# An encoder layer on one core: weights traced two pairs ahead, the up projection in the order of the source, and the heavy pair first in the last block

## The chip, the cores and the metric

The kernel runs on one core of one Trainium2 chip. The metric is the device time of one execution in microseconds (us): 1366.28, the median of three runs from 1365.36 to 1366.99. The engines are PE (TensorE), DVE (VectorE), ACT (ScalarE), POOL (GpSimd) and SP (SyncE, which here only issues transfers).

## The reference

One layer of a bidirectional encoder for 256 tokens and a model width of 2048, in float32: a combined input projection, two attention branches with sigmoid gates, an output projection with a residual, and an MLP of width 8192 with a squared ReLU.

```python
proj = jnp.einsum('bsd,dc->bsc', rms_norm(x, norm_mix_pre[l]), w_in[l])
qa, ka, va, qn, kn, vn, gates = jnp.split(proj, split_at, axis=-1)
...
g_a, g_b = jnp.split(jax.nn.sigmoid(gates), N_BRANCHES, axis=-1)
mixed = (g_a * jnp.einsum('bsc,cd->bsd', oa, w_branch_a[l])
         + g_b * jnp.einsum('bsc,cd->bsd', on, w_branch_b[l]))
y = jnp.einsum('bsd,de->bse', mixed, w_out[l])
x = x + rms_norm(y, norm_mix_post[l])
h = rms_norm(x, norm_mlp_pre[l])
u = jnp.square(jax.nn.relu(jnp.einsum('bsd,df->bsf', h, w_up[l])))
x = x + rms_norm(jnp.einsum('bsf,fd->bsd', u, w_down[l]), norm_mlp_post[l])
```

## The kernel before

Every matrix product is made of three: operands are split into a high part (float32r) and a low part, and high x high, high x low and low x high are summed in PSUM. `pair_weights` (L602) loads 1 MB of weights, a *pair* of row blocks by 1024 columns, into `raw`, casts it to the high part on ACT (tiles ending in `h`, L609) and subtracts to get the low part on DVE (`l`, L610). Raw, high and low tiles have three slots each. A name such as `u_1h` is the high part of pair 1 of the up projection `u`; with numbers kept, `u2_1h` belongs to its third group.

A pair is used in one of two ways (`Products`, L632). A *plain* pair takes 24 matmuls of 512 columns (`eight`). A *heavy* pair is multiplied with seven products instead of eight (`seven`, L655): 21 matmuls, but DVE must first make sums of its blocks (`t`, L614 to L616) and split these too (`eh`, `el`, L626 and L627). Its products go to sums numbered 0 to 6 in PSUM, which `combine` (L673) joins at the end. Sums 1, 2, 3 and 7 have four banks of their own; sums 0, 4, 6 and 5 share four small banks (pool `ms`) with the transposes.

The up projection (L1030 to L1062) has eight groups of 1024 columns with eight pairs each. The first group takes plain pairs only; it begins while the residual of the stage ahead is still being made: `residual_parts` (L865) computes `x` on DVE, PE transposes it (`h2T_t`), and ACT and DVE write the high and low part of the pieces `h2T` (L885, L886) that the pairs are multiplied with. The other groups have two heavy pairs. While a group runs, the result of the one before is transposed on PE (`uT`, L1014, four banks in all, two for each half), squared on ACT (L1017), split into `ah` and `al`, with sums `sm` for the heavy use, and stored to DRAM (`u_sets`, L1006).

The down projection (L1105 to L1164) makes two halves of 1024 output columns from blocks of four pairs; the saved parts come back through ACT's queue as `bh` and `bl` (L989). A pair `d1131` is half 1, column group 13, part 1. The last block of a half ends with combining the heavy sums into `zw` (L677 to L680), adding the plain sums, and in the second half scaling and storing the result.

A scheduler sets the order of each engine's instructions: it goes by the order in which they are traced and by which it expects to be ready. `issue_after` keeps an instruction behind another one of its engine. Only the last blocks of the down projection have PE in the order of the source (`pr.in_order`, L1114).

## Time and profile before

| | |
|---|---|
| median of three runs | 1366.28 us |
| profiled execution, own time | 1367.36 us |
| its span, first to last instruction | 1365.5 us |
| mean granted clock of TensorE | 0.995 |
| stages: input projection and attention / gates and branches | to about 305 / 305 to 568 us |
| output projection / up / down | 568 to 658 / 658 to 1016 / 1016 to 1354 us |

The page has the busy time of each engine, a chain followed back from the last instruction, and groups of instructions with their mean duration and the idle time before them. Matmuls overlap, so the pace is read from starts. The granted clock is the share of TensorE's full clock that the throttle let through. Lines like L649 are lines of the kernel before.

### The profile page before, as it was taken

What the parts mean: (1) busy time and instruction counts of PE and PEld (TensorE: products, weight loads), DVE (VectorE), ACT (ScalarE), POOL (GpSimd) and SP (SyncE); (2) the same over time, 40 slices, a digit from 0 to 9 for tenths busy, and PEclk for the clock granted to TensorE, in tenths of its full rate; (3) what the DMA queues carried; (4) which work ended last, traced back from release to release, by engine and by line L of the source; (5) the groups of instructions that cost most, each with busy time, mean ns of one, the idle gap of its engine ahead of it and who ended that gap; (6) DMA issues with size and microseconds to landing.
All of it is one profiled execution on the core that took longest, in us unless ns stands there. A gap on an engine that the chain in (4) does not pass through costs nothing.

```text
span 1365.5 us, 16240 instructions
## 1 busy us (share of the span) xinstructions
PE 1341.8 (98%) x6350; PEld 1122.6 (82%) x6350; DVE 1030.8 (75%) x1176; ACT 716.4 (52%) x841; POOL 36.2 (3%) x71
## 2 busy tenths in 40 slices
PE   7999999999999999999999999999999999999995
PEld 6888888888888888888788888888888888888884
DVE  6868866667857886654768877888788888798885
ACT  7555455555644464444465655666555555555451
POOL 0000000000000000000100000000000000000000
PEclk9999999999999999999999999999999999999997
DMA  9674745564556655676567776786699999698992
GB/s 310 201 227 165 205 158 178 163 206 154 185 186 215 216 185 185 205 265 203 197 206 268 252 245 244 258 280 238 249 339 356 374 353 358 248 387 310 373 356 75
DMA packets 116397, 333.76 MB, mean 244 GB/s; under 512 B 17248, under 2 KB 18528, under 8 KB 116320
## 3 DMA queue, kind: packets, MB, share of 16 engines
q1 hardware_dynamic: 96784, 264.03, 56.7%
q10 hardware_dynamic: 12816, 43.01, 8.1%
q0 software_dynamic: 6720, 25.69, 4.8%
q8 instruction: 50, 0.82, 0.2%
q14 instruction: 27, 0.22, 0.0%
HBM read 304.91 MB, written 29.61 MB: 245 GB/s over the span
## 4 chain that ended last, share of the span: by engine, by line
PE 61%; issue 34%; DVE 2%; DMA 2%; ACT 1%; ACTq 0%; SPq 0%; POOL 0%; DVEq 0%; POOLq 0%
PE u L649 25%; PE p L649 22%; PE qa_p L192 2%; PE ka_p L192 2%; DMA bl<-keepl 1%; PE qa_p L193 1%; PE ka_p L193 1%; PE qn_p L192 1%; PE va_p L230 1%; PE va_p L231 1%; PE va_p L232 1%; PE uT L1014 1%; PE qn_p L193 1%; PE ds L378 0%; PE do L378 0%
## 5 line engine op out<-in xcount | busy, mean ns | idle before, releaser
L117 DVE TENSOR_TENSOR y_l<-y_w,y_h 128x1024 fp32r<-128x1024 f32 x32 | 37.9, 1222 | 31.0 <-ACT y_h L116 31.0
L116 ACT CAST y_h<-y_w 128x1024 fp32r<-128x1024 f32 x32 | 32.1, 1052 | 40.9 <-PE y_p L232 32.5
L230 PE MATMUL y_p<-y_h,mh 128*128 128x512 f32 x128 | 50.1, 391 | 0.0
L231 PE MATMUL y_p<-y_l,mh 128*128 128x512 f32 x128 | 49.9, 390 | 0.0
L232 PE MATMUL y_p<-y_h,ml 128*128 128x512 f32 x128 | 49.8, 390 | 0.0
L192 PE MATMUL qa_p<-hT,qa_h 128*128 128x512 f32 x128 | 46.9, 411 | 1.2 <-DVE hT L275 1.2
L649 PE MATMUL u<-u_0h,h2T 128*128 128x512 f32 x128 | 44.6, 392 | 2.3 <-DVE ry_m L86 1.1
L192 PE MATMUL qn_p<-hT,qn_h 128*128 128x512 f32 x128 | 45.9, 400 | 0.0
L192 PE MATMUL kn_p<-hT,kn_h 128*128 128x512 f32 x128 | 45.4, 398 | 0.0
L192 PE MATMUL ka_p<-hT,ka_h 128*128 128x512 f32 x128 | 45.0, 398 | 0.0
L649 PE MATMUL u<-u_1h,h2T 128*128 128x512 f32 x128 | 44.6, 395 | 0.0
L649 PE MATMUL u<-u_4h,h2T 128*128 128x512 f32 x128 | 42.1, 390 | 0.0
L649 PE MATMUL u<-u_2h,h2T 128*128 128x512 f32 x128 | 41.9, 397 | 0.0
L649 PE MATMUL u<-u_6h,h2T 128*128 128x512 f32 x128 | 41.8, 389 | 0.0
L649 PE MATMUL u<-u_7h,h2T 128*128 128x512 f32 x128 | 41.0, 389 | 0.0
L193 PE MATMUL qn_p<-hT,qn_l 128*128 128x256 f32 x128 | 35.9, 281 | 0.0
L193 PE MATMUL kn_p<-hT,kn_l 128*128 128x256 f32 x128 | 35.7, 280 | 0.0
L193 PE MATMUL qa_p<-hT,qa_l 128*128 128x256 f32 x128 | 35.2, 285 | 0.0
L193 PE MATMUL ka_p<-hT,ka_l 128*128 128x256 f32 x128 | 35.2, 280 | 0.0
L609 ACT CAST u_1h<-u_1r 128x2048 fp32r<-128x2048 f32 x8 | 15.3, 1917 | 36.0 <-PE u L649 32.5
L649 PEld LDWEIGHTS u<-u_0h,h2T 128*128 128x128 f32 x128 | 23.9, 188 | 8.4 <-DVE ry_m L86 1.6
L192 PEld LDWEIGHTS qa_p<-hT,qa_h 128*128 128x128 f32 x128 | 24.5, 194 | 6.6 <-DVE hT L275 1.6
(1376 smaller groups left out, 4351.2 us busy)
## 6 DMA issues: line engine op xcount, KB each, us to landing
y_w<-in_w_out SPq DMA_DIRECT2D x16, 1024.0 KB, 5.2
bh<-keeph ACTq DMA_DIRECT2D x30, 512.0 KB, 9.6
bl<-keepl ACTq DMA_DIRECT2D x30, 512.0 KB, 11.6
keeph<-ah POOLq DMA_DIRECT2D x18, 512.0 KB, 3.5
keepl<-al POOLq DMA_DIRECT2D x18, 512.0 KB, 7.2
ka_w<-in_w_in SPq DMA_DIRECT2D x8, 1024.0 KB, 5.7
va_w<-in_w_in SPq DMA_DIRECT2D x8, 1024.0 KB, 5.1
qn_w<-in_w_in SPq DMA_DIRECT2D x8, 1024.0 KB, 5.2
```

Of the source, the lines that this page charges most:

```text
L116: nc.scalar.copy(hi[part], raw[part])
L117: nc.vector.tensor_sub(lo[part], raw[part], hi[part].bitcast(F32))
L192: nc.tensor.matmul(ps[b], hi[:, k % 4, cs], mv, start=(k == 0), stop=False)
L193: nc.tensor.matmul(ps[b][:, :T], lo[:, k % 4, cs], mv[:, :T], start=False, stop=(k == nk - 1))
L230: nc.tensor.matmul(ps[t], sh, hi[:, k % 4], start=(k == 0), stop=False)
L231: nc.tensor.matmul(ps[t], sh, lo[:, k % 4], start=False, stop=False)
L232: nc.tensor.matmul(ps[t], sl, hi[:, k % 4], start=False, stop=(k == nk - 1))
L609: nc.scalar.copy(h1, raw)
L649: ins = nc.tensor.matmul(self.ps[i], st, mv[:, blk], start=i not in self.begun, stop=last and n == 2).ins
L1014: nc.tensor.transpose(pt[:, j * T + t * P : j * T + (t + 1) * P], z[t][:, cg % 2, c : c + P], ident)
```

## The change

Weights are asked for in a list ahead of the loop, one list for gates and branches (`gw`), one for the up and down projections together (`uw`). `next` hands out one pair and has the two behind it traced first, so that their load, cast and subtraction are traced ahead of the work in between; that work (`each`) now comes behind the call. In `seven`, sum 0 moves behind 2 and 1. In the up projection the heavy pairs are 0 and 3 (before 3 and 5), at the third and fifth place (before fourth and sixth), and PE keeps the order of the source from the second group on. In the first group the low parts of pairs 1 and 2 are put behind named instructions of DVE. The last block of each half of the down projection begins with its heavy pair.

```diff
-    def pair_weights(view, name, seven, low=None):
+    def pair_weights(view, name, seven, low=None, after=None):
...
-            nc.vector.tensor_sub(l1, raw, h1.bitcast(F32))
+            with tc.issue_after(after) if after else nullcontext():
+                nc.vector.tensor_sub(l1, raw, h1.bitcast(F32))
...
+    class Weights:
...
+        def next(self, after={}):
+            i = self.used = getattr(self, "used", -1) + 1
+            upto = min(i + 3, len(self.asked), self.stop or len(self.asked))
+            for n in range(len(self.got), max(upto, i + 1)):
+                self.got.append(pair_weights(*self.asked[n], after=after.get(n)))
+            w, self.got[i] = self.got[i], None
+            return w
...
-            self.add(0, stat(0), r, 1, last)
             self.add(2, stat(6), r, 2)
             self.add(1, stat(1), r, 3)
+            self.add(0, stat(0), r, 1, last)
...
+        pr.in_order = in_order
         for n, (i, seven) in enumerate(kinds):
+            w = weights.next(after)
             if each:
                 each(n)
-            w = pair_weights(view(i), f"{name}_{i}", seven)
...
-    UPS = [(0, 0), (1, 0), (2, 0), (3, 1), (4, 0), (5, 1), (6, 0), (7, 0)]
+    UPS = [(1, 0), (2, 0), (0, 1), (4, 0), (3, 1), (5, 0), (6, 0), (7, 0)]
...
+    def down_steps(g, bi):
+        b = blocks[g][bi]
+        if bi == 0:
+            return [(b + 1, 0, 0), (b, 1, 0), (b, 0, g), (b + 1, 1, 0)]
+        return [(b, 0, 1), (b + 1, 0, 0), (b, 1, bi < len(blocks[g]) - 1), (b + 1, 1, 0)]
...
-                    for i in (3, 5):
+                    for i in (0, 3):
...
-            turn=None if g else partial(residual_parts, 1, 0),
+            turn=None if g else turn_rows,
+            after={} if g else {1: tail[1][1], 2: scaled[0]},
+            in_order=g > 0,
...
-            elif end:
-                steps = [(b + 1, 0, 0), (b, 0, 1), (b, 1, 0), (b + 1, 1, 0)]
-                pr.in_order = True
...
+            pr.in_order = end
```

(`tail[1][1]` is the last low piece of `residual_parts` for the first 128 tokens, `scaled[0]` the scaling `ry_m` for the second 128.)

PE in the third group of the up projection, where the heavy pair's sums begin (`u20` to `u27` are the sums of this group; `uT30` and `uT31` are transposes of the second half of the group before). Before:

```order
L649 MATMUL u20_6347<-u2_5h_6404,h2T5_4852 128x512 [waits Activation_49]
L649 MATMUL u22_6190<-u2_5h_6404,h2s5_5798 128x512
L649 MATMUL u21_6183<-u2_5h_6404,h2T5_4852 128x512
L649 MATMUL u24_6357<-u2_3eh0_6339,h2s3_5787 128x512 [waits PE_49,Activation_49]
L649 MATMUL u26_6361<-u2_3eh0_6339,h2s3_5787 128x512
L649 MATMUL u20_6347<-u2_5l_6405,h2T5_4852 128x512 [waits DVE_49]
L649 MATMUL u20_6347<-u2_5h_6404,h2T5_4852 128x512
L649 MATMUL u22_6190<-u2_5l_6405,h2s5_5798 128x512
L649 MATMUL u22_6190<-u2_5h_6404,h2s5_5798 128x512
L649 MATMUL u21_6183<-u2_5l_6405,h2T5_4852 128x512
L649 MATMUL u21_6183<-u2_5h_6404,h2T5_4852 128x512
```

Now:

```order
L686 MATMUL u20_6346<-u2_0h_6189,h2T0_4847 128x512 [waits Activation_49]
L686 MATMUL u20_6346<-u2_0l_6190,h2T0_4847 128x512
L686 MATMUL u20_6346<-u2_0h_6189,h2T0_4847 128x512
L686 MATMUL u24_6350<-u2_0eh0_6198,h2s0_5803 128x512 [waits Activation_49]
L686 MATMUL u24_6350<-u2_0el0_6199,h2s0_5803 128x512
L686 MATMUL u24_6350<-u2_0eh0_6198,h2s0_5803 128x512
L686 MATMUL u26_6354<-u2_0eh0_6198,h2s0_5803 128x512 [waits PE_49,Activation_49]
L686 MATMUL u26_6354<-u2_0el0_6199,h2s0_5803 128x512
L686 MATMUL u26_6354<-u2_0eh0_6198,h2s0_5803 128x512
L686 MATMUL u25_6358<-u2_0eh1_6202,h2s0_5803 128x512 [waits PE_49,Activation_49]
L686 MATMUL u25_6358<-u2_0el1_6203,h2s0_5803 128x512
```

In both built programs sum 6 (`u26`) takes the bank of `uT30` and waits for PE and ACT. Before, some 47 matmuls, of two plain pairs and of both heavy ones, stood between the last of the four transposed banks and sum 4 (`u24`) with sum 6 behind it; now twelve matmuls of the heavy pair stand between the transposes and sum 6.

ACT in the same group, from the cast of the pair `u2_3` to the squares of the second half, `u3<-uT30` and `u3<-uT31`. Before:

```order
L613 CAST u2_3h_6330<-u2_3r_6328 128x1536 [waits DMAHW3_49,PE_49,Activation_49]
L1017 ACTIVATE u2_6211<-uT20_6212 128x512 [waits PE_49]
L1017 ACTIVATE u2_6211<-uT21_6218 128x512 [waits PE_49]
L972 CAST ah20_6229<-u2_6211 128x256 [waits Activation_49]
L972 CAST ah20_6229<-u2_6211 128x512 [waits Activation_49]
L972 CAST ah21_6239<-sm2_6224 128x1024 [waits DMASW5_49,DMASW1_49,DVE_49]
L609 CAST u2_4h_6374<-u2_4r_6372 128x2048 [waits DMAHW4_49,PE_49]
L1017 ACTIVATE u3_6277<-uT30_6278 128x512 [waits DMASW6_49]
L1017 ACTIVATE u3_6277<-uT31_6284 128x512 [waits PE_49]
L972 CAST ah30_6290<-u3_6277 128x1024 [waits Activation_49]
L613 CAST u2_5h_6404<-u2_5r_6402 128x1536 [waits DMAHW5_49,PE_49]
L626 CAST u2_3eh0_6339<-u2_3t0_6332 128x1024 [waits DVE_49]
```

Now, from the same cast:

```order
L629 CAST u2_3h_6302<-u2_3r_6300 128x1536 [waits DMAHW4_49,PE_49]
L1026 CAST ah21_6268<-sm2_6253 128x1024 [waits DMASW1_49,DVE_49]
L624 CAST u2_5h_6367<-u2_5r_6365 128x2048 [waits DMAHW5_49,PE_49]
L642 CAST u2_3eh0_6311<-u2_3t0_6304 128x1024 [waits DVE_49]
L1071 ACTIVATE u3_6319<-uT30_6320 128x512
L1071 ACTIVATE u3_6319<-uT31_6326 128x512
L1026 CAST ah30_6332<-u3_6319 128x1024 [waits Activation_49]
L642 CAST u2_3eh1_6315<-u2_3t1_6305 128x1024 [waits DVE_49,PE_49]
```

The cast of the pair `u2_5` and the first cast of a heavy pair's block sums, `u2_3eh0`, stood behind the two squares and now stand ahead of them.

DVE at the begin of the up projection, behind the four instructions that make `x` of the first 128 tokens (the rows before and now). Before:

```order
L610 TENSOR_TENSOR u_1l<-u_1r,u_1h 128x2048
L886 SCALAR_TENSOR_TENSOR h2T_4847<-h2T_t_5393,g_mlp,h2T_4847 128x128
L886 SCALAR_TENSOR_TENSOR h2T_4848<-h2T_t_5400,g_mlp,h2T_4848 128x128
L886 SCALAR_TENSOR_TENSOR h2T_4849<-h2T_t_5411,g_mlp,h2T_4849 128x128
L886 SCALAR_TENSOR_TENSOR h2T_4850<-h2T_t_5418,g_mlp,h2T_4850 128x128
L918 TENSOR_TENSOR yw_4840<-y_p_5264,gpost_4826 128x512
L862 TENSOR_REDUCE sy_5434<-ssy_4842 128x1
L610 TENSOR_TENSOR u_2l<-u_2r,u_2h 128x2048
L886 SCALAR_TENSOR_TENSOR h2T_4847<-h2T_t_5393,g_mlp,h2T_4847 128x128
L86 TENSOR_SCALAR ry_m<-sy_5434 128x1
L886 SCALAR_TENSOR_TENSOR h2T_4848<-h2T_t_5400,g_mlp,h2T_4848 128x128
L886 SCALAR_TENSOR_TENSOR h2T_4849<-h2T_t_5411,g_mlp,h2T_4849 128x128
```

Now, from the second piece `h2T` on, since the first follows `x` directly:

```order
L932 SCALAR_TENSOR_TENSOR h2T_4848<-h2T_t_5400,g_mlp,h2T_4848 128x128
L932 SCALAR_TENSOR_TENSOR h2T_4849<-h2T_t_5411,g_mlp,h2T_4849 128x128
L932 SCALAR_TENSOR_TENSOR h2T_4850<-h2T_t_5418,g_mlp,h2T_4850 128x128
L932 SCALAR_TENSOR_TENSOR h2T_4847<-h2T_t_5393,g_mlp,h2T_4847 128x128
L932 SCALAR_TENSOR_TENSOR h2T_4848<-h2T_t_5400,g_mlp,h2T_4848 128x128
L932 SCALAR_TENSOR_TENSOR h2T_4849<-h2T_t_5411,g_mlp,h2T_4849 128x128
L972 TENSOR_TENSOR yw_4840<-y_p_5264,gpost_4826 128x512
L908 TENSOR_REDUCE sy_5434<-ssy_4842 128x1
L932 SCALAR_TENSOR_TENSOR h2T_4850<-h2T_t_5418,g_mlp,h2T_4850 128x128
L626 TENSOR_TENSOR u_1l<-u_1r,u_1h 128x2048
L98 TENSOR_SCALAR ry_m<-sy_5434 128x1
L626 TENSOR_TENSOR u_2l<-u_2r,u_2h 128x2048
```

The low part of pair 1 moves from ahead of all pieces to behind them, and that of pair 2 behind the scaling `ry_m`.

DVE in the last block of the second half, from the heavy pair's last low part on. Before:

```order
L627 TENSOR_TENSOR d1120el1_10603<-d1120t1_10592,d1120eh1_10602 128x1024
L610 TENSOR_TENSOR d1121l_10637<-d1121r_10634,d1121h_10636 128x2048
L677 TENSOR_TENSOR zw10_10627<-zw10_10627,p15_9592 128x512
L678 TENSOR_TENSOR zw11_10628<-zw10_10627,p16_9588 128x512
L679 TENSOR_TENSOR zw10_10627<-p14_9584,zw10_10627 128x512
L680 TENSOR_TENSOR zw11_10628<-p14_9584,zw11_10628 128x512
L610 TENSOR_TENSOR d1131l_10643<-d1131r_10640,d1131h_10642 128x2048
```

Now:

```order
L643 TENSOR_TENSOR d1120el1_10518<-d1120t1_10507,d1120eh1_10517 128x1024
L626 TENSOR_TENSOR d1121l_10577<-d1121r_10574,d1121h_10576 128x2048
L714 TENSOR_TENSOR zw10_10609<-zw10_10609,p15_9617 128x512
L715 TENSOR_TENSOR zw11_10610<-zw10_10609,p16_9613 128x512
L626 TENSOR_TENSOR d1131l_10619<-d1131r_10616,d1131h_10618 128x2048
L716 TENSOR_TENSOR zw10_10609<-p14_9609,zw10_10609 128x512
L717 TENSOR_TENSOR zw11_10610<-p14_9609,zw11_10610 128x512
```

The low part of `d1131` moves from behind the combination (`zw`) into its middle; on PE the block's heavy pair now comes ahead of three plain ones, before it came second.

More of the change, by code (lines that the diff above doesn't have):

```diff
@@ L35, with __init__, __getitem__ @@
 TC = dict(schedule_with_timeline_sim=True)
+class Late:
+    def __init__(self, make):
+        self.make, self.made = make, None
+    def __getitem__(self, i):
+        if self.made is None:
+            self.made = self.make()
+        return self.made[i]
 @with_exitstack
@@ L85, in inv_rms @@
         ms_ = small(w, f"{name}_m")
-        nc.vector.tensor_scalar(ms_, ss, 1.0 / n, EPS, op0=ALU.mult, op1=ALU.add)
+        scaled[0] = nc.vector.tensor_scalar(
+            ms_, ss, 1.0 / n, EPS, op0=ALU.mult, op1=ALU.add
+        ).ins
         if r is None:
@@ L93, in encoder_layer @@
     last_load = [None]
+    scaled = [None]
     def load(src, k0, nk, c0, cw, name):
@@ L628, in pair_weights, with __init__, ask, columns @@
         return h1, l1, h2, l2
+    class Weights:
+        def __init__(self):
+            self.asked, self.got, self.stop = [], [], None
+        def ask(self, *args):
+            self.asked.append(args)
+        def next(self, after={}):
[5 more added lines that the diff above has]
+            return w
+    def columns(src, i, c):
+        return src[i * T : (i + 1) * T, c : c + 1024].rearrange("(k p) c -> p k c", p=P)
     PLAIN = ((1, 0, 1), (2, 0, 0), (3, 1, 1), (7, 1, 0))
@@ L680, in combine, with wide_group @@
             nc.vector.tensor_sub(c22, self.ps[4], c21)
-    def wide_group(name, kinds, view, stat7, stat8, mm_banks, z, piece, each=None, turn=None):
+    def wide_group(name, kinds, weights, stat7, stat8, mm_banks, z, piece, each=None, turn=None, after={}, in_order=False):
         any7 = any(s for _, s in kinds)
         pr = Products(name, mm_banks)
+        pr.in_order = in_order
         for n, (i, seven) in enumerate(kinds):
+            w = weights.next(after)
             if each:
                 each(n)
-            w = pair_weights(view(i), f"{name}_{i}", seven)
             if seven:
@@ L752, in encoder_layer @@
     mixed = []
+    gw = Weights()
+    for h in range(2):
+        for nm, src, c, kinds in (
+            ("ga", w_in, GA, MIXED if h else ALL8),
+            ("gb", w_in, GB, MIXED),
+            ("ba", a["w_branch_a"], 0, ALL8[:4]),
+            ("bb", a["w_branch_b"], 0, ALL8[:4]),
+        ):
+            for i, seven in kinds:
+                gw.ask(columns(src, i, c + h * 1024), f"{nm}{h}_{i}", seven)
+    gw.stop = 8
     def mixed_T(h, n):
@@ L795, in encoder_layer @@
                 ALL8 if first_one else MIXED,
-                lambda i, c=gc + h * 1024: w_in[i * T : (i + 1) * T, c : c + 1024].rearrange(
-                    "(k p) c -> p k c", p=P
-                ),
+                gw,
                 hstat7,
@@ L809, in encoder_layer @@
                 mid = ctx.enter_context(tc.tile_pool(name="mid", bufs=5, reuse_waits="tile"))
+                gw.stop = None
             gate.append(z)
@@ L821, in encoder_layer @@
                 ALL8[:4],
-                lambda i, src=src, c=h * 1024: src[i * T : (i + 1) * T, c : c + 1024].rearrange(
-                    "(k p) c -> p k c", p=P
-                ),
+                gw,
                 None,
@@ L894, in residual_parts, with turn_rows @@
         return last.ins, act.ins, vec.ins
+    tail = []
     def between(i):
-        return residual_parts(0, i - 5)[0] if i in (5, 6) else None
+        if i in (5, 6):
+            last, act, vec = residual_parts(0, i - 5)
+            tail.append((act, vec))
+            return last
+    def turn_rows():
+        residual_parts(1, 0)
     def mlp_squares(t):
@@ L1028, in u_piece @@
         nc.scalar.activation(zt, zt if summed else ps, AF.Relu, scale=r2[:, t : t + 1])
-    UPS = [(0, 0), (1, 0), (2, 0), (3, 1), (4, 0), (5, 1), (6, 0), (7, 0)]
+    UPS = [(1, 0), (2, 0), (0, 1), (4, 0), (3, 1), (5, 0), (6, 0), (7, 0)]
+    uw = Weights()
+    for g in range(DFF // 1024):
+        for i, seven in UPS if g else ALL8:
+            uw.ask(columns(a["w_up"], i, g * 1024), f"u{g}_{i}", seven)
+    wd = a["w_down"].rearrange("(g h j p) c -> p h g j c", h=2, j=2, p=P)
+    blocks = [[NG - 4] + list(range(0, NG - 4, 2)) + [NG - 2], [NG - 2] + list(range(0, NG - 2, 2))]
+    def down_steps(g, bi):
[3 more added lines that the diff above has]
+        return [(b, 0, 1), (b + 1, 0, 0), (b, 1, bi < len(blocks[g]) - 1), (b + 1, 1, 0)]
+    for g in range(2):
+        for bi in range(len(blocks[g])):
+            for cg, j, seven in down_steps(g, bi):
+                uw.ask(wd[:, :, cg, j, g * 1024 : (g + 1) * 1024], f"d{g}{cg}{j}", seven, page)
     uz = None
     for g in range(DFF // 1024):
-        z = [page([P, 2, 512], F32, f"u{g}{t}") for t in range(2)]
+        z = Late(lambda g=g: [page([P, 2, 512], F32, f"u{g}{t}") for t in range(2)])
         def up_each(n, g=g, uz=uz):
@@ L1050, in encoder_layer @@
             UPS if g else ALL8,
-            lambda i, c=g * 1024: a["w_up"][i * T : (i + 1) * T, c : c + 1024].rearrange(
-                "(k p) c -> p k c", p=P
-            ),
+            uw,
             h2stat7,
@@ L1059, in encoder_layer @@
             each=up_each,
-            turn=None if g else partial(residual_parts, 1, 0),
+            turn=None if g else turn_rows,
+            after={} if g else {1: tail[1][1], 2: scaled[0]},
+            in_order=g > 0,
         )
         uz = z
-    wd = a["w_down"].rearrange("(g h j p) c -> p h g j c", h=2, j=2, p=P)
     def dstat7(sets, j, n):
@@ L1102, in finish @@
             nc.sync.dma_start(out[t * P : (t + 1) * P, c * 512 : (c + 1) * 512], z)
-    blocks = [[NG - 4] + list(range(0, NG - 4, 2)) + [NG - 2], [NG - 2] + list(range(0, NG - 2, 2))]
     for g in range(2):
@@ L1109, in encoder_layer @@
             end = bi == len(blocks[g]) - 1
-            if bi == 0:
-                steps = [(b + 1, 0, 0), (b, 1, 0), (b, 0, g), (b + 1, 1, 0)]
-            elif end:
-                steps = [(b + 1, 0, 0), (b, 0, 1), (b, 1, 0), (b + 1, 1, 0)]
-                pr.in_order = True
-            else:
-                steps = [(b, 0, 1), (b + 1, 0, 0), (b, 1, 1), (b + 1, 1, 0)]
-            for n, (cg, j, seven) in enumerate(steps):
-                w = pair_weights(wd[:, :, cg, j, g * 1024 : (g + 1) * 1024], f"d{g}{cg}{j}", seven, page)
+            pr.in_order = end
+            for n, (cg, j, seven) in enumerate(down_steps(g, bi)):
+                w = uw.next()
                 if g == 0 and bi == 0 and n in (1, 2):
```

## The prediction

> **What bounds the kernel now.** I read the page first, then the waits of TensorE (PE), then windows around each wait, and last the groups and the timeline of VectorE (DVE) and ScalarE (ACT) there. The page:

> ```profile
> span 1365.5 us, 16240 instructions
> PE 1341.8 (98%) x6350; PEld 1122.6 (82%) x6350; DVE 1030.8 (75%) x1176; ACT 716.4 (52%) x841; POOL 36.2 (3%) x71
> ...
> L649 PE MATMUL u<-u_0h,h2T 128*128 128x512 f32 x128 | 44.6, 392 | 2.3 <-DVE ry_m L86 1.1
> ```

> PE is busy for 98% of the span. The reader should take from it that little can be gained: a change that only moves instructions can win what PE waits, and can lose as much as it makes PE wait. The last row, a group of matmuls, has 0.39 us for one and 2.3 us of idle time before them. So I ask where PE waits (line, releaser: total, times, longest):

> ```profile
> PE p L649 <- DVE d1131l L610: 2.8, 1, 2.8
> PE u L649 <- DVE ry_m L86: 1.1, 1, 1.1
> PE u L649 <- ACT h2T L885: 0.9, 1, 0.9
> PE u L649 <- DVE h2T L886: 0.3, 1, 0.3
> PE p L649 <- ACT d021eh L626: 0.3, 1, 0.3
> ```

> Three waits stand where the up projection begins, one early in the down projection, one in its last block. The windows show what they cost (busy time and count of each engine, the granted clock, DMA share, GB/s):

> ```profile
> core 0: us, PE busy (x) PEld busy (x) DVE busy (x) ACT busy (x) POOL busy (x), PEclk, DMA share, GB/s
> 658.30:664.30 6.00, 3.69 (x15) 2.08 (x14) 6.00 (x13) 3.52 (x7) 0.52 (x1) 1.00 0.84 295
> 720.70:764.70 44.00, 44.00 (x204) 36.50 (x203) 35.78 (x34) 26.12 (x26) 3.23 (x6) 1.00 0.73 257
> 1066.50:1337.00 270.50, 270.44 (x1193) 224.03 (x1194) 225.59 (x184) 139.72 (x111) 0.00 (x0) 1.00 0.88 338
> 1338.90:1342.10 3.20, 0.40 (x2) 0.00 (x0) 3.17 (x3) 0.00 (x0) 0.00 (x0) 0.91 0.01 3
> 1342.10:1348.30 6.20, 6.17 (x15) 4.88 (x16) 1.38 (x2) 0.72 (x2) 0.00 (x0) 0.50 0.01 3
> 1348.30:1354.60 6.30, 6.30 (x28) 4.89 (x26) 4.28 (x9) 1.45 (x4) 0.56 (x1) 1.00 0.07 27
> ```

> One group of the up projection (second row, 44.0 us) has PE busy throughout. After the wait in the last block the clock is 0.50 for 6.2 us: 15 matmuls start there, 28 in the next 6.3 us. Two pieces of the chain that ended last give the undisturbed pace:

> ```profile
> 719.84 0.87 PE uT L1014 x8
> 720.71 37.68 PE u L649 x166
> ```

> That is 37.68/166 = 0.227 us from one matmul of 512 columns to the next and 0.109 per transpose. A matmul's record (0.39) ends 0.16 behind the point where the next could have begun, so each wait costs 0.16 more than the view says.

> **The begin of the up projection.** DVE's timeline there (start, duration, instruction):

> ```profile
> 654.50 2.74 DVE L869 SCALAR_TENSOR_TENSOR x<-yw,ry,x 128x512 f32<-128x512 f32 x4 [0.67 <-POOL ry L89]
> 657.16 2.29 DVE L610 TENSOR_TENSOR u_1l<-u_1r,u_1h 128x2048 fp32r<-128x2048 f32 x1
> 659.36 1.12 DVE L886 SCALAR_TENSOR_TENSOR h2T<-h2T_t,g_mlp,h2T 128x128 fp32r<-128x128 f32 x4
> 660.39 0.69 DVE L918 TENSOR_TENSOR yw<-y_p,gpost 128x512 f32<-128x512 f32 x1
> 661.08 2.29 DVE L610 TENSOR_TENSOR u_2l<-u_2r,u_2h 128x2048 fp32r<-128x2048 f32 x1
> ```

> Two low parts of 2.29 us stand ahead of the 128-column pieces h2T that PE waits for. The three waits lose 2.3 + 3 x 0.16 = 2.8 us; in the window 6.0/0.227 = 26 matmuls would fit and 15 were counted, which is 2.5. Now seven pieces come first: 657.16 + 7 x 0.27 = 659.1, so PE's twelve matmuls with u_0 (658.3 + 12 x 0.227 = 661.1) don't wait. Then product, reduction and the eighth piece (about 1 us), and u_1l from 660.1 to 662.3, while PE wants it two matmuls after 661.1, at 661.5. A new wait of 0.7 us, up to 1.2 if ACT's pieces lag, is what is late next. u_2l follows directly and is ready when wanted. Term: 0.7 - 2.8 = **-2.1 us** (bounds -2.8 and -1.3).

> **The up groups after the first.** This is where I see the price. Rows of the trace of before for one group (line, engine, names: busy, mean ns):

> ```profile
> L973 DVE TENSOR_TENSOR al<-sm,ah 128x1024 fp32r<-128x1024 f32 x2 | 2.4, 1222 | 1.1 <-ACT ah L972 1.1
> L617 DVE TENSOR_TENSOR u_3l<-u_3r,u_3h 128x1536 fp32r<-128x1536 f32 x1 | 1.8, 1758 | 2.1 <-ACT u_3h L613 2.1
> L614 DVE TENSOR_TENSOR u_3t<-u_3r 128x1024 f32<-128x1024 f32 x1 | 1.2, 1218 | 0.0
> L609 ACT CAST u_4h<-u_4r 128x2048 fp32r<-128x2048 f32 x2 | 3.8, 1906 | 2.0 <-PE u L649 2.0
> L1017 ACT ACTIVATE u<-uT 128x512 f32<-128x512 f32 x4 | 2.2, 591 | 0.8 <-PE uT L1014 0.8
> L626 ACT CAST u_3eh<-u_3t 128x1024 fp32r<-128x1024 f32 x2 | 2.1, 1046 | 0.1
> L613 ACT CAST u_3h<-u_3r 128x1536 fp32r<-128x1536 f32 x1 | 1.5, 1474 | 2.0 <-issue 2.0
> ```

> Four small PSUM banks serve both the transposes of the previous group's result (uT, four banks) and the sums 0, 4, 6 and 5 of a heavy pair. Before, the first heavy pair came fourth and the scheduler let other matmuls go ahead of its sums 4 and 6, some 47 behind the transposes (10.7 us), so a bank that came late held up nobody. Now the heavy pair is third, right behind the last transposes, and each matmul of the group stands behind the one ahead of it in the source. Sum 6 takes the bank of uT30 (its first matmul waits for PE and ACT in the order shown above), which is free when ACT has squared uT30. On ACT that square now stands behind u_3h, the cast of the sums, u_5h and u_3eh; u_3eh needs u_3t from DVE, and on DVE u_3t stands behind u_3l and the low part of the sums.

> u_3h can't start early: with three slots it takes the one of u_2, the second pair, so it starts when PE ends that pair. Call this moment 0. The chain: u_3h 1.47, u_3l 1.76, low part of the sums 1.22, u_3t 1.22, u_3eh 1.05, square 0.59, together 7.31. Neighbours on one engine overlap by 0.08 (654.50 + 2.74 against 657.16 in the timeline), three times, and three handovers between engines give about that back: 7.2 to 7.3. u_5h is off this path: it waits for u_0's slot until 2.7 and ends at 4.6, ahead of u_3t at 5.6. PE in the meantime has six transposes (0.65) and twelve matmuls of the heavy pair (sums 2, 1, 0, 4: 2.72), less the 0.16 by which the end of the last matmul lags: it runs dry at 3.2. The wait is 4.0 us, and since it is counted from PE's own step it comes back in each of the seven groups: 7 x 4.0 = **+28 us**. Bounds: 0 if the square were free at 3.2, 7 x 5 = 35 with 1 us of slower handovers; I take the sum of the rows.

> **The clock behind each wait.** The wait of 2.8 us in the last block was followed by 0.50 for 6.2 us, where 27 matmuls would fit and 15 ran: 12 x 0.227 = 2.7 us. The row 658.30 shows gaps of at most about 1.3 us and the clock at 1.00. A gap of 3.9 us lies beyond the longer of the two, so I expect the drop each time: 7 x 2.7 = **+19 us**, bounds 0 and 7 x 3.4 (6.8 us cold). [...]

> **The last block.** DVE ahead of the wait:

> ```profile
> 1337.14 0.69 DVE L677 TENSOR_TENSOR zw<-zw,p 128x512 f32<-128x512 f32 x1 [4.17 <-PE p L649]
> 1337.87 0.69 DVE L678 TENSOR_TENSOR zw<-zw,p 128x512 f32<-128x512 f32 x1
> 1338.59 0.69 DVE L679 TENSOR_TENSOR zw<-p,zw 128x512 f32<-128x512 f32 x1
> 1339.20 0.68 DVE L680 TENSOR_TENSOR zw<-p,zw 128x512 f32<-128x512 f32 x1
> 1339.79 2.28 DVE L610 TENSOR_TENSOR d1131l<-d1131r,d1131h 128x2048 fp32r<-128x2048 f32 x1
> ```

> The heavy pair first means that 24 more matmuls (5.4 us) stand between its combination and the pair 1131, and DVE now makes d1131l between the two halves of the combination. The wait (2.8 + 0.16 = 3.0 us) and its cold stretch (2.7) go. What is late next is a load: the block's saved activations, whose second half the heavy pair wants at once and the plain pair didn't.

> ```profile
> bl<-keepl ACTq DMA_DIRECT2D x30, 512.0 KB, 11.6
> ```

> With 11.6 us to landing (median) this may cost 0 to 5.4 us; the middle blocks begin with their heavy pair too and show no wait in 270.5 us, so I take 0.8. Term: **-4.9 us**. Early in the down projection the same kind of wait may grow from 0.3 to 0.7: **+0.4**.

> **Nothing for the longer list.** Three slots of raw, high and low hold the loads to the same places as before; the SP queue changes in the order of pairs alone. Moved casts and low parts are as many and as long as before; PE's 44.0 us a group cover DVE's 35.8 and ACT's 26.1. Without that cover (PE waiting) they cost what is counted above.

> **Sum.** The profiled execution took 1367.36 us (1.08 above the median of the runs, 1366.28). 1367.36 - 2.1 + 28 + 19 - 4.9 + 0.4 = 1407.8; less 1.08 gives 1406.7, rounded to **1407**.

> **Rivals.**
> - *Waits without the clock drop*, or with a drop now and then, if the clock falls only when a gap happens to fill a whole stretch over which PE's work is counted: 1407 - 19 = 1388, to 1397 with half of the drops. For it: the clock stayed at 1.00 at 658.30. Against: the drop after 2.8 us. 0.14. [...]
> - *No wait in the groups, faster*: if ACT's square of uT30 ran early, or u_3h started before PE ended u_2. It decides at 3.2 us behind that end: a square done by then costs nothing, and 1366.28 - 2.1 - 4.9 + 0.4 = 1359.7 remains. For it: before, the same banks and engines never made PE wait in these groups. Against: the queue's order is fixed, and 7.2 us of rows stand ahead of the square. 0.08.
> - *The change does nothing that matters*: loads stay where the slots put them, and the gains are eaten by short waits, 1364 to 1369. 0.03.
> - *Loads too late as well*: stalls as forecast, and the down projection (DMA share 0.88) waits for saved activations in more blocks, from 1413 on. 0.05.

> My forecast has 0.70. The range 1388 to 1413 takes in the forecast with its bounds and the first rival. Faster by over 0.2% (2.7 us, about what a measurement of this kernel can tell from no change) 0.08, within it 0.03, slower 0.89.

> **What would show it.** Seven waits of PE of about 4 us, one in each group from 717 us on, 48 to 51 us apart, each ended by ACT's square of uT and standing at the heavy pair's fifth sum (6); the granted clock at 0.50 for some 3.4 to 6.8 us behind each; at the begin of the up projection one short wait for u_1l in place of three; no wait for d1131l and no cold stretch near the end. I am wrong if a group still takes 44 us, if the square of uT30 starts earlier than 6 us behind the end of the second pair, or if the clock stays at 1.00.

## The result and the profile after

The changed kernel takes 1408.2 us (median of four runs, 1406.75 to 1410.11) against 1366.26 before (median of four, beside it): 1.0308 times as long, 95% interval 1.029 to 1.0326. Its profiled execution took 1410.11 us, 42.75 more than that of before. The page of the changed kernel:

```profile
span 1408.3 us, 16222 instructions
PE 1358.9 (96%) x6350; PEld 1131.6 (80%) x6350; DVE 1030.0 (73%) x1176; ACT 719.5 (51%) x841; POOL 38.1 (3%) x71
```

No engine has noticeably more work (the same 6350 matmuls and transposes, DVE 1030.0 us against 1030.8, ACT 719.5 against 716.4). PE waits more, and it is busy for 17 us longer, since its matmuls take longer where the granted clock is 0.50: behind the first gap (728.15 to 730.28) a record of 512 columns takes 0.63 us and the starts lie 0.43 apart, at 1.00 it is 0.39 and 0.227. The waits of PE in the changed kernel (line, releaser: total, times, longest):

```profile
PE u L686 <- ACT u L1071: 26.7, 7, 3.9
...
PE p L686 <- DMA bl<-keepl: 1.6, 2, 0.9
PE p L686 <- DMA bh<-keeph: 1.4, 2, 0.8
...
PE u L686 <- DVE ry_m L98: 0.8, 1, 0.8
```

Seven waits for ACT's square of uT (line 1071 now) have come, and four short ones for saved activations; that for `d1131l` has gone. The short wait at the begin of the up projection stands at a matmul with `u_1l`; the view puts it down to `ry_m`, the next instruction on DVE. ACT and DVE of the changed kernel in the second up group, the first in which PE keeps the order of the source (start, duration, instruction, idle time and its releaser):

```profile
719.11 1.48 ACT L629 CAST u_3h<-u_3r 128x1536 fp32r<-128x1536 f32 x1 [2.37 <-PE u L686]
720.49 1.04 ACT L1026 CAST ah<-sm 128x1024 fp32r<-128x1024 f32 x1
721.75 1.90 ACT L624 CAST u_5h<-u_5r 128x2048 fp32r<-128x2048 f32 x1 [0.22 <-PE u L686]
724.68 1.04 ACT L642 CAST u_3eh<-u_3t 128x1024 fp32r<-128x1024 f32 x1 [1.03 <-DVE u_3t L630]
725.63 1.08 ACT L1071 ACTIVATE u<-uT 128x512 f32<-128x512 f32 x2
```

```profile
720.62 1.76 DVE L633 TENSOR_TENSOR u_3l<-u_3r,u_3h 128x1536 fp32r<-128x1536 f32 x1 [0.95 <-ACT u_3h L629]
722.30 1.22 DVE L1027 TENSOR_TENSOR al<-sm,ah 128x1024 fp32r<-128x1024 f32 x1
723.43 1.22 DVE L630 TENSOR_TENSOR u_3t<-u_3r 128x1024 f32<-128x1024 f32 x1
```

And PE, the last matmul ahead of the gap and the first behind it:

```profile
722.01 0.39 PE L686 MATMUL u<-u_0eh,h2s 128*128 128x512 f32 x1
726.28 0.79 PE L686 MATMUL u<-u_0eh,h2s 128*128 128x512 f32 x1 [3.88 <-ACT u L1071]
```

The reader can follow the chain from the cast u_3h at 719.11 over three steps of DVE and back to ACT until the square, and PE starts 0.65 us behind the square's start. From 719.1 to 726.3 are 7.2 us. What each place costs is seen in windows (us, busy time and count of PE, PEld, DVE, ACT, POOL, the granted clock, DMA share, GB/s):

```profile
659.00:665.00 6.00, 5.15 (x23) 3.96 (x22) 5.79 (x10) 3.11 (x6) 1.55 (x1) 1.00 0.43 143
721.39:724.81 3.42, 1.01 (x5) 0.50 (x3) 3.42 (x4) 2.17 (x3) 1.07 (x2) 1.00 0.97 368
724.81:731.63 6.82, 5.35 (x13) 4.19 (x14) 6.74 (x6) 4.00 (x5) 1.06 (x2) 0.50 0.74 243
731.63:772.59 40.96, 40.96 (x190) 33.89 (x189) 26.10 (x26) 20.64 (x20) 1.18 (x3) 1.00 0.59 199
1104.00:1114.00 10.00, 7.90 (x31) 5.10 (x31) 9.83 (x11) 6.06 (x6) 0.00 (x0) 1.00 1.02 408
1372.00:1380.00 8.00, 7.09 (x32) 5.55 (x31) 6.61 (x4) 4.36 (x4) 0.00 (x0) 1.00 1.03 408
```

The third row is the clock's drop: 13 matmuls start in 6.82 us, where the pace allows 30; 1.47 us of that are still the gap. The fifth is the begin of the down projection (31 starts, 44 would fit), the sixth is the last block: one short gap, the clock at 1.00.

To add this up over a whole execution I take, from the trace, the distance of each matmul's start to the next and subtract the pace (0.227 us for 512 columns, 0.109 per transpose). What is left is the time lost by stage:

| profiled execution | own time | ahead of up | begin of up | up groups | begin of down | last block |
|---|---|---|---|---|---|---|
| before | 1367.36 | 12.1 | 3.2 | 0.7 | 0.6 | 5.9 |
| changed | 1410.11 | 12.8 | 1.25 | 46.6 | 3.3 | 1.3 |
| difference | +42.75 | +0.7 | -1.95 | +45.9 | +2.8 | -4.6 |

Of the 46.6 in the groups 27.9 are the seven gaps and about 18 the slow stretches behind them (five of 6.8 us and two of 3.4 in the records of the clock).

### The profile page after: what moved, and what is told of

Its sections match the earlier page's. It is cut to its first block, busy times and chain, and to the rows that moved or that the text cites. A ratio compares the mean times of both kernels' runs of the same rounds, so it can differ in the third digit from the quotient of the medians.

```text
span 1408.3 us, 16222 instructions
## 1 busy us (share of the span) xinstructions
PE 1358.9 (96%) x6350; PEld 1131.6 (80%) x6350; DVE 1030.0 (73%) x1176; ACT 719.5 (51%) x841; POOL 38.1 (3%) x71
## 4 chain that ended last, share of the span: by engine, by line
PE 89%; DVE 4%; DMA 3%; ACT 2%; issue 1%; ACTq 0%; SPq 0%; DVEq 0%; POOLq 0%
PE u L686 22%; PE p L686 20%; PE ga L686 6%; PE gb L686 6%; PE ba L686 3%; PE bb L686 3%; PE qa_p L207 2%; PE ka_p L207 2%; PE qn_p L207 2%; PE kn_p L207 2%; PE y_p L246 2%; PE y_p L245 2%; PE y_p L247 2%; PE qa_p L208 1%; PE qn_p L208 1%
## 5 line engine op out<-in xcount | busy, mean ns | idle before, releaser
L132 DVE TENSOR_TENSOR y_l<-y_w,y_h 128x1024 fp32r<-128x1024 f32 x32 | 37.9, 1222 | 30.9 <-ACT y_h L131 30.9
L626 DVE TENSOR_TENSOR u_6l<-u_6r,u_6h 128x2048 fp32r<-128x2048 f32 x8 | 18.3, 2293 | 48.8 <-ACT u_6h L624 48.8
L686 PE MATMUL u<-u_0eh,h2s 128*128 128x512 f32 x42 | 22.1, 558 | 26.7 <-ACT u L1071 26.7
L207 PE MATMUL qn_p<-hT,qn_h 128*128 128x512 f32 x128 | 45.9, 400 | 0.0
L686 PE MATMUL u<-u_4h,h2T 128*128 128x512 f32 x128 | 45.0, 422 | 0.0
L686 PE MATMUL u<-u_5h,h2T 128*128 128x512 f32 x128 | 40.7, 389 | 0.0
L624 ACT CAST u_6h<-u_6r 128x2048 fp32r<-128x2048 f32 x8 | 15.3, 1912 | 43.5 <-PE u L686 42.7
L686 PEld LDWEIGHTS u<-u_0eh,h2s 128*128 128x128 f32 x42 | 11.1, 265 | 32.1 <-ACT u L1071 29.7
L626 DVE TENSOR_TENSOR u_4l<-u_4r,u_4h 128x2048 fp32r<-128x2048 f32 x8 | 18.3, 2292 | 24.4 <-ACT u_4h L624 24.4
## 6 DMA issues: line engine op xcount, KB each, us to landing
bh<-keeph ACTq DMA_DIRECT2D x30, 512.0 KB, 9.9
bl<-keepl ACTq DMA_DIRECT2D x30, 512.0 KB, 11.8
keeph<-ah POOLq DMA_DIRECT2D x18, 512.0 KB, 5.2
keepl<-al POOLq DMA_DIRECT2D x18, 512.0 KB, 6.0
```

What stands on the lines that cost most here:

```text
L132: nc.vector.tensor_sub(lo[part], raw[part], hi[part].bitcast(F32))
L207: nc.tensor.matmul(ps[b], hi[:, k % 4, cs], mv, start=(k == 0), stop=False)
L624: nc.scalar.copy(h1, raw)
L626: nc.vector.tensor_sub(l1, raw, h1.bitcast(F32))
L686: ins = nc.tensor.matmul(self.ps[i], st, mv[:, blk], start=i not in self.begun, stop=last and n == 2).ins
```

## The experiments

Medians are of 4 to 11 executions, in e6_zero8 and e11_not_ahead of two; ratios are against the kernel before on the same chip. The column "profiled" is the time of the execution that was traced, and the three stages behind it are the time lost in that execution, in the order of the text:

| run | median | ratio (95%) | profiled | up groups | begin of down | last block |
|---|---|---|---|---|---|---|
| e1_place | 1365.79 | 0.9993 (0.9984 to 1.0003) | 1363.48 | 3.8 | 1.6 | 1.1 |
| e2_free | 1369.4 | 1.0021 (1.0012 to 1.003) | 1369.4 | 9.4 | 0.7 | 1.1 |
| e5_each | 1386.85 | 1.0157 (1.014 to 1.0173) | 1390.98 | 26.9 | 3.4 | 1.0 |
| e3_zero16 | 1391.43 | 1.018 (1.0165 to 1.0195) | 1389.64 | 4.2 | 1.1 | 1.4 |
| e4_zero4 | 1398.46 | 1.024 (1.0221 to 1.0258) | 1396.69 | 29.8 | 0.5 | 1.4 |
| e6_zero8 | 1394.12 | 1.0205 (1.0186 to 1.0223) | 1393.97 | 20.3 | 1.5 | 1.5 |
| e7_last | 1362.16 | 0.9972 (0.9961 to 0.9983) | 1362.16 | 0.7 | 0.9 | -0.1 |
| e8_both | 1360.0 | 0.9957 (0.9943 to 0.997) | 1359.31 | 0.7 | 0.8 | -0.1 |
| e9_loads | 1363.82 | 0.9981 (0.9972 to 0.999) | 1364.55 | 2.9 | 2.6 | -0.1 |
| e10_place_free | 1366.0 | 1.0005 (0.9993 to 1.0017) | 1368.81 | 4.3 | 4.0 | 1.1 |
| e12_free_not_ahead | 1360.8 | 0.9958 (0.9945 to 0.9972) | 1360.91 | 0.7 | 0.6 | -0.1 |
| e11_not_ahead | 1421.21 | 1.0404 (1.0385 to 1.0423) | 1421.71 | 60.7 | 3.2 | -0.1 |

### What makes the seven waits

**The place of the heavy pair** (e1_place, on the changed kernel):

```diff
-    UPS = [(1, 0), (2, 0), (0, 1), (4, 0), (3, 1), (5, 0), (6, 0), (7, 0)]
+    UPS = [(1, 0), (2, 0), (4, 0), (0, 1), (5, 0), (3, 1), (6, 0), (7, 0)]
```

> The changed kernel with the two heavy pairs of each up group back at the fourth and sixth place; all else stays (the list two pairs ahead, PE in the order of the source, the last block). Theory of the prediction: the heavy pair right behind the transposes is what makes PE wait for the square of uT; one plain pair more ahead of it (24 matmuls, 5.4 us) covers the 4.0 us, so the seven waits and the slow clock behind them go. In the changed kernel they make 46.5 us over the pace of 0.227 us (27.9 in the gaps, 18.6 in the slow stretches), so 1408.2 - 46.5 = 1361.7, between 1359 and 1365, granted clock 1.00 in all up groups. Rival, the order of the source itself is the cost: seven waits of over 1 us stay somewhere in the groups, 1375 to 1405. Rival, weights traced two pairs ahead are the cost (casts ahead of squares): the same, since they are still traced ahead.

The seven waits for the square and the slow clock are gone from the groups (granted clock 1.00 from 670 to 1020 us), 46.6 to 3.8 us: one plain pair more ahead of the heavy one is cover enough. What came in their place in the waits of this kernel:

```profile
PE u L686 <- DVE u L1081: 2.0, 3, 1.5
```

With 1365.8 it is 4 us above what was expected and no faster than before. These 4 us are taken up below.

**PE's order** (e2_free, on the changed kernel):

```diff
-            in_order=g > 0,
+            in_order=False,
```

> The changed kernel without PE's order of the source in the up groups; the heavy pairs stay third and fifth. Theory of the prediction: each matmul stands behind the one ahead of it, so a bank that comes late holds up all; freed, other matmuls can go ahead of sum 6, and most of the 46.5 us go: short waits of 0 to 2.7 us in some groups, 1361 to 1372. Rival, the place alone is enough (the square of uT is late whatever PE's order): seven waits of about 4 us stay, 1395 to 1410.

1369.4, as the theory said. The waits for the square are gone with the heavy pairs still third and fifth; three waits for another low part have come, the longest of 2.5 us, and the mean clock of this execution is 0.996, against 0.997 in e1:

```profile
PE u L686 <- DVE u_1l L626: 5.5, 3, 2.5
```

So it takes both: the heavy pair right behind the transposes, and an order in which nothing can go ahead of its sums.

**ACT's order** (e5_each, on the changed kernel):

```diff
-            w = weights.next(after)
             if each:
                 each(n)
+            w = weights.next(after)
```

> The changed kernel with the work in between (transposes, squares and splits of the group before) traced ahead of the call for the next weights, in place of behind it; heavy pairs third and fifth and PE's order as in the changed kernel. The built order then has the squares of uT30 and uT31 on ACT ahead of u_3h, the low parts of the sums and u_3eh. Theory of the prediction (the square is late because casts and splits of a pair two ahead stand in front of it): the seven waits of 4.0 us for the square go, 1408.2 - 46.5 = 1361.7. What is late next by the built order and the rows: the last low part of the second heavy pair (u_3el), now behind that work on DVE, 2.0 to 2.3 us in each group, 7 x 2.1 = 15; with the slow clock behind some of these gaps (up to 7 x 2.7): 1377 to 1390. Rival, sum 6 waits for its bank whatever ACT's order: the waits of 4 us for the square stay, 1400 to 1410.

1386.9. With the squares ahead of the casts, the waits for the square are gone. The waits of this kernel name the successor that was expected, 2.0 us by starts in each group:

```profile
PE u L686 <- DVE u_3el L643: 12.9, 7, 1.8
```

This shows that sum 6 was held by what stands ahead of the square on ACT, and not by its bank as such. The 26.9 us that stay in the groups are 14 us of gaps and 12.9 of the slow clock, which fell behind all seven in this execution (1.8 us for each; with starts 0.43 us apart in place of 0.227, as in the changed kernel, 3.41 us lose 1.6). It is the longest of four: the others took 1385.65 to 1387.19 us at a mean clock of 0.990 to 0.992, against 0.989 here, so in them the clock was low for less time.

### What the clock costs

In e3_zero16 sixteen matmuls with a block of zeros stand in the gap, in e4_zero4 four, in e6_zero8 eight (on the changed kernel; `zero` is made once by subtracting `ident` from itself):

```diff
+        def fill(self):
+            for _ in range(16 if self.name[0] == "u" and self.begun.isdisjoint({6}) else 0):
+                with tc.issue_after(self.after):
+                    self.after = nc.tensor.matmul(self.ps[3], zero, hT2[7][:, 0], start=False, stop=False).ins
...
             self.add(4, stat(3), t[0], 0, last)
+            self.fill()
             self.add(6, stat(4), t[0], 1, last)
```

> The changed kernel with sixteen matmuls more in each up group from the second on, between sums 4 and 6 of the first heavy pair: an all-zero stationary block is multiplied with a tile that is long there and added to sum 3, which adds nothing. They take 16 x 0.227 = 3.6 us of the 4.0 us in which PE waits, and nothing waits for them but sum 6. So the wait as a delay stays and PE is busy in it. Theory of the prediction (the slow clock behind the wait is a cost of its own): granted clock 1.00 in all up groups, waits of 0.3 to 0.5 us, and 1408.2 - 18.6 = 1389.6 us (1387 to 1392) with 112 matmuls more. Rival, the clock does not matter (the stretch behind the wait is slow for another reason, as weights or sums that come late): 1408 as before. Rival, the wait is not set by the chain on ACT but counts from PE's last matmul: 112 x 0.227 = 25 us more, 1430.

With 112 matmuls more the kernel is 16.8 us faster than the changed one (1391.4 against 1408.2). Window of this kernel over the groups:

```profile
670.00:1070.00 400.00, 399.44 (x1819) 327.87 (x1818) 293.80 (x298) 226.50 (x236) 25.86 (x48) 1.00 0.69 240
```

The clock is 1.00 throughout. In the table 4.2 us stay in the groups beside 112 x 0.227 = 25.4 us of zeros: together 29.6, the waits as a delay. The other 17 of the changed kernel's 46.6 were the clock.

> As the kernel with sixteen matmuls of zeros, but with four in each group: the gap shrinks from 4.0 to 3.1 us, seven times, each at another phase of the clock's grid (the events of the granted clock lie on multiples of 3.41 us: 13.7, 1341.5, 1348.3, 1358.6). Theory of the prediction (the clock fell after a wait of 2.8 us in the kernel before): the drop comes again behind all or most of the seven, 1404 to 1409. Rival, the clock falls only behind a gap that fills a whole stretch of the grid of 3.41 us: no drop, granted clock 1.00, 1387 to 1392. [...]

1398.5, between the two ranges: in the profiled execution the clock fell behind four of the seven gaps of 3.04 us, for 3.4 us each time (mean clock 0.992, against 0.998 in e3). Neither theory had that. The number is not the same in every execution: two of the four took 1396.7 and 1396.8 us at a mean clock of 0.992, the other two 1400.1 and 1401.2 at 0.988. Two gaps of the same length in this kernel, laid on the clock's grid (in the traces of before and of the changed kernel, the changes of the clock lie whole multiples of 3.413 us apart: before, 13.72, 1341.51, 1348.34 and 1358.58):

```profile
820.00:823.41 3.41, 1.10 (x5) 0.56 (x3) 3.41 (x4) 2.46 (x3) 0.61 (x2) 1.00 1.00 411
823.41:826.83 3.42, 2.86 (x7) 2.28 (x8) 3.27 (x4) 2.06 (x4) 0.53 (x1) 0.50 0.68 217
918.99:922.40 3.41, 1.60 (x7) 0.94 (x6) 3.41 (x4) 2.45 (x2) 1.08 (x2) 1.00 1.00 388
922.40:925.82 3.42, 2.36 (x10) 1.95 (x11) 3.42 (x4) 2.55 (x4) 0.53 (x1) 1.00 0.74 241
```

The first lies within one stretch (PE busy 1.10 us of 3.41) and the next is at 0.50; the second is split between two (1.60 and 2.36) and the clock stays at 1.00. Neither stretch is without work.

> As the kernels with sixteen and four matmuls of zeros, but with eight in each group: gaps of 2.1 us. Sixteen (gap 0.3) left the granted clock at 1.00, four (gap 3.04) let it fall behind four of the seven gaps. If the clock falls where one stretch of the grid (3.41 us) holds too little work, the number of drops falls with the gap: 0 to 2 of 7, 1390 to 1395. Rival, any gap above the 1.4 us of the kernel before can do it, by phase alone: again 3 to 5 of 7, 1396 to 1400.

1394.1: two of seven (the stretches from 822.99 and 1017.55 are at 0.50), as the theory by the work in a stretch said. These are two executions, 1393.97 and 1394.27 us, both at a mean clock of 0.995.

### The two parts that gain

e7_last edits the kernel before:

```diff
-                steps = [(b + 1, 0, 0), (b, 0, 1), (b, 1, 0), (b + 1, 1, 0)]
+                steps = [(b, 0, 1), (b + 1, 0, 0), (b, 1, 0), (b + 1, 1, 0)]
```

> The kernel before with one edit: the last block of each half of the down projection begins with its heavy pair. Theory of the prediction: the wait for d1131l (3.0 us) and the cold stretch behind it (2.7) go; in the kernel before the saved activations are asked for ahead of the casts of the pairs two ahead, so the wait of 1.1 us for them that the changed kernel shows there is smaller or absent: -4.6 to -5.9, 1360.3 to 1361.9. Rival, as in the changed kernel the load takes part of it back: -4.6. Rival, the wait for DVE moves to another pair of the block: -1 to -3.

1362.2, 3.8 us below the kernel before beside it (1365.95). In the profile 5.9 us go from the last block and nothing comes in their place; the median gains less than the profile.

e8_both puts the begin of the up projection beside it, again on the kernel before (`tail` and `scaled` as in the change):

```diff
-            nc.vector.tensor_sub(l1, raw, h1.bitcast(F32))
+            with tc.issue_after(after) if after else nullcontext():
+                nc.vector.tensor_sub(l1, raw, h1.bitcast(F32))
...
+            after={} if g else {1: tail[1][1], 2: scaled[0]},
```

> The kernel before with two parts of the change: the last block begins with its heavy pair, and in the first up group the low parts of pairs 1 and 2 stand behind the named instructions of DVE. The up groups, the tracing of weights and PE's order are those of the kernel before. Theory of the prediction: the begin of the up projection gains what the changed kernel shows there (3.3 us over the pace before, 1.3 now, so -1.9), the last block -4.6 to -5.9: 1358.5 to 1360, faster than both. Rival, the gain at the begin needs the weights to be traced ahead: -4.6 to -5.9 alone, as in the kernel with the last block's edit.

1360.0, a ratio of 0.9957 (0.9943 to 0.997): faster than the kernel before, by 0.4%, and than the changed one. Against e7_last, 2.2 us lower. In its waits one short one stands at the begin, the same as in the changed kernel, at `u_1l` again:

```profile
PE u L651 <- DVE ry_m L86: 0.8, 1, 0.8
```

### What the list two pairs ahead costs

e1_place and e8_both differ by 5.8 us in the medians, by 5.2 if each is taken against the kernel before beside it. Four runs take it apart.

e9_loads is e1_place with the loads of the saved activations traced ahead of the weights:

```diff
-                w = uw.next()
+                if n:
+                    w = uw.next()
...
                             sets[1, b + c] = sets[0, b + c]
+                    w = uw.next()
```

> The kernel with the heavy pairs back at the fourth and sixth place (1365.8) with one more edit: in the down projection the loads of the saved activations are traced ahead of the call for the next weights, in place of behind it, so that ACT issues them ahead of the casts of the pairs two ahead. Theory: these casts wait for their own loads and hold back the issue of the saved activations; that is the 1.6 us over the pace at the begin of the down projection and the 1.2 us in the last block, against 0.6 and nothing in the kernels without the list. They go, so -2.2: 1363 to 1364. Rival, the transfers themselves are late since all queues are full there (DMA share 1.02 from 1100 to 1115 in the changed kernel): no gain, 1365 to 1367.

1363.8, by the size as expected (against the kernel before, 2.6 us are gained in place of 0.8), but half of the way is another. The wait in the last block is gone (1.1 to -0.1). At the begin of the down projection the waits for the loads went, and a wait for a split of a heavy pair came instead, so that 2.6 us stand there:

```profile
PE p L686 <- ACT d020eh L642: 1.3, 1, 1.3
```

e10_place_free is e1_place with `in_order=False`.

> The kernel with the heavy pairs back at the fourth and sixth place (1365.8), without PE's order of the source in the up groups. Theory: of the 5.8 us between it and the kernel before with begin and last block alone (1360.0), some 3 are lost at the begin of up groups, where PE in the order of the source waits for DVE to empty a bank (u, line 1081), and DVE stands at a sum of a pair two ahead whose load has not landed; freed, PE takes other matmuls first: 1362 to 1364. Rival, the weights traced two pairs ahead are the cost whatever PE's order: 1365 to 1367.

1366.0: the rival. PE's order is not what costs here. The timeline of DVE in e1_place shows what does, at the longest wait of its groups:

```profile
835.91 1.23 DVE L630 TENSOR_TENSOR u_0t<-u_0r 128x1024 f32<-128x1024 f32 x1 [2.09 <-DMA u_0r<-in_w_up]
837.06 2.28 DVE L626 TENSOR_TENSOR u_2l<-u_2r,u_2h 128x2048 fp32r<-128x2048 f32 x1
839.26 0.68 DVE L1081 TENSOR_TENSOR u<-u,u 128x512 f32<-128x512 f32 x1
```

DVE idles 2.09 us at a sum of the heavy pair three places on, whose load has not landed, and the emptying of a bank (L1081), for which PE waits, stands behind it. In e10, with PE free, DVE meets the same load at the same group and PE waits 1.5 us again:

```profile
840.52 1.23 DVE L630 TENSOR_TENSOR u_0t<-u_0r 128x1024 f32<-128x1024 f32 x1 [2.27 <-DMA u_0r<-in_w_up]
```

e12_free_not_ahead is e10_place_free with no pair traced ahead from the second up group on:

```diff
-            upto = min(i + 3, len(self.asked), self.stop or len(self.asked))
+            upto = min(i + (3 if i < 8 or self is gw else 1), len(self.asked), self.stop or len(self.asked))
...
-            w = weights.next(after)
             if each:
                 each(n)
+            w = weights.next(after)
```

> The kernel with the heavy pairs back and PE free in the up groups (1366.0), with no pair traced ahead from the second up group on, and the work in between traced ahead of the weights. Of the change there remain the begin of the up projection, the last block, the list in the stages ahead, and the order of plain pairs and sums. Theory: the 6.0 us between 1366.0 and 1360.0 (the kernel before with begin and last block alone) are the price of tracing two pairs ahead where the order is the scheduler's: waits at the begin of groups for DVE, and saved activations issued late; without it 1359 to 1361. Rival, they come from something else of the change (the list in the stages ahead, the order of plain pairs and sums): 1364 to 1367.

1360.8: the 5 us are the price of tracing ahead, with which both edits, taken together, do away from the second group on. By stage it goes from the groups, the begin of the down projection and the last block. The rest of the change (the list in the stages ahead, the order of plain pairs and of sums) costs nothing that these runs can tell.

e11_not_ahead has the same edit with PE in the order of the source:

> The kernel with the heavy pairs back at the fourth and sixth place (1365.8), with no pair traced ahead from the second up group on (the work in between is traced ahead of the weights too, as in the kernel before); PE stays in the order of the source in the up groups. Theory: under the order of the source the list two pairs ahead is what brings the casts and sums early enough; without it the built order has the heavy pairs' splits behind the work in between, and PE waits in each group some 0.6, 3.5, 0.9 and 2.5 us, 7 x 7.5 = 52 us, and the slow clock behind the longer ones (7 x 2.7): 1418 to 1440. Rival, tracing ahead only costs: 1360 to 1364.

1421.2, within what was expected, 60.7 us in the groups; the waits are 38 us by the view and not 52, the rest is in the main the slow clock (mean 0.982, against 0.997 in e1). The waits:

```profile
PE u L686 <- DVE u_0el L643: 34.5, 14, 3.2
PE u L686 <- ACT u_0eh L642: 3.5, 7, 0.6
```

Under the order of the source the list is needed; where the scheduler orders PE it is not, and only its price is left.

## Why the prediction was right, point by point

- **The sum.** Forecast 1407 (range 1388 to 1413, and 0.89 for slower), measured 1408.2. The likeliest case came. Part of the closeness is chance. For the profiled execution the forecast was 1407.8 and 1410.11 was measured: 2.4 us too little at the begin of the down projection, 1.1 too much in the groups, and 0.7 ahead of the up projection, whose first matmul starts between 657.1 and 659.9 us in the fourteen profiles. The median lies 1.9 us below that execution.
- **The seven group waits**, +28 forecast: 27.9 by starts. The chain of 7.2 to 7.3 us measures 7.2 (719.1 to 726.3) and stands in the forecast order. e1, e2 and e5 show the three conditions that the working named, each by taking one away: the place, the fixed order, and what stands ahead of the square on ACT.
- **The clock behind each wait**, +19 forecast at 2.7 a wait: about 18, shown apart from the waits by e3 (16.8 by the medians). The number is right, but the reason for "each time" was too short. One drop behind a wait of 2.8 us was taken to mean that 3.9 must always do it; in e4 gaps of 3.04 us did it four times in seven in one execution. That 3.9 us did it seven times in seven agrees with the estimate in the last section. The first rival, that the gap has to fill a whole stretch, disagrees with these traces: the stretch of 3.41 us ahead of the drop at 724.81 holds 1.01 us of work.
- **The begin of the up projection**, -2.1 forecast: -1.95 in the profile, -2.2 between e8 and e7. The new wait is 1.0 us by starts at `u_1l`, in the forecast 0.7 to 1.2.
- **The last block**, -4.9 forecast: -4.6 in the profile, with the late load at 1.1 us instead of 0.8. The reason given for this load was wrong: in e7 the heavy pair is first too and wants both halves of the saved activations at once, but without the list nothing is lost there (-0.1). It is the list that makes the load late, as at the begin of the down projection below. The profiled execution of before was one with a low clock: its mean was 0.995, and in the 19 runs of it beside e1 the clock was 0.995 to 0.997, the time 1364.33 us in the shortest, at 0.997, and 1368.56 in the longest, at 0.995. That suggests that the wait of 2.8 us does not bring the slow stretch each time, so that the median had less to gain (-3.8 in e7); no second trace of this kernel shows it.
- **The begin of the down projection**, +0.4 forecast: +2.8. This is the term that was wrong, with the part headed "Nothing for the longer list": the 0.4 was for a wait for a split of a heavy pair, and the loads of the saved activations were put at nothing. The saved activations are issued by ACT, and the list puts casts of later pairs ahead of their issue. In the changed kernel:

```profile
1095.18 1.05 ACT L642 CAST d001eh<-d001t 128x1024 fp32r<-128x1024 f32 x1 [3.67 <-DVE d001t L630]
1096.14 1.48 ACT L629 CAST d020h<-d020r 128x1536 fp32r<-128x1536 f32 x1
...
1098.92 1.92 ACT L624 CAST d030h<-d030r 128x2048 fp32r<-128x2048 f32 x1 [0.37 <-DMA d030r<-in_w_down]
1098.94 0.33 ACTq L1043 DMA_DIRECT2D bh<-keeph  x1
```

The issue stands behind casts of the later pairs `d020` and `d030`, and behind a split that waited 3.67 us for DVE; the wait of `d030h` for its own load is the smallest part, 0.37 us. PE came to the first of these activations at 1105.15, 6 us on, and the first wait that the view names for them ended at 1107.41:

```profile
1105.15 0.50 PE L686 MATMUL p<-d020h,bh 128*128 128x512 f32 x1
...
1107.41 0.50 PE L686 MATMUL p<-d020h,bh 128*128 128x512 f32 x1 [0.54 <-DMA bh<-keeph]
```

In the kernel before the first of them was issued at 1041.18 and used at 1060.20, 19 us on:

```profile
1041.18 0.39 ACTq L989 DMA_DIRECT2D bh<-keeph  x1
```

```profile
1060.20 0.39 PE L649 MATMUL p<-d020h,bh 128*128 128x512 f32 x1
```

The transfers themselves are no slower: in these stretches the loads `bh` take 8.2 us from issue to landing (median), before 8.3.

The prediction had looked at SP's queue alone. Its rival "loads too late as well" named the right kind of wait, but not its size or place: 3 us at the begin and 1 in the last block, and none in the middle blocks.

- **The rival "faster"** needed a square done 3.2 us behind the second pair's end. e1 shows what it would have given without the group waits: 1365.8, and not the 1359.7 worked out, since the list's own price of 5 us was missing there too. The early square did not come: that of `uT30` started at 725.63, 6.5 us behind the start of u_3h.

## What to carry to other kernels

On an engine that is 98% busy, an order written by hand takes away the slack that let other work slip ahead of a late buffer (1408.2 us, and 1369.4 with PE free in e2): walk the chain that frees each buffer on the *other* engines, and count it against the instructions that are left ahead of its next use. Work traced ahead moves more than its loads: whatever shares a queue with its casts, an emptying of a bank or the issue of another load, gets behind a wait for data that it does not need (2.09 us on DVE in e1, 3.67 us on ACT in the changed kernel). And a change of five parts is best timed part by part: two of these five are worth 6 us, and were buried under 46.
